# A two-layer trunk on one core: sums over channel tiles and every fifth tap added by accumulating transfers inside SBUF

## The chip, the cores and the metric

The kernel runs on one core of a Trainium2 chip. The metric is the device time of one execution in microseconds (us). The kernel before takes 1701.81 us, the median of three runs (1701.59 to 1702.53).

## The reference

The reference is a decoder trunk of two layers over 1024 tokens of 1024 channels, all in float32. Layer 0 mixes tokens by a causal depthwise convolution, layer 1 by a chunked spatial gate; behind each layer a per-layer embedding is added through a sigmoid gate, and one last RMSNorm ends it.

```python
for i in range(2):
    h = rmsnorm(x, norm_g[i])
    a, b, z = split(h @ w_in[i], 3)            # 3 x 2048 channels
    if i == 0:                                  # convolution layer
        y = a * sigmoid(b)
        y = causal_depthwise_conv(y, conv_w, 31 taps) + conv_b
        y = silu(layernorm(y))                  # over the 2048 channels
    else:
        y = gelu(a) * (w_s @ layernorm(gelu(b)) + b_s)   # in chunks of 128 tokens
    x = x + (y * silu(z)) @ w_out[i]
    x = x + sigmoid(rmsnorm(x) @ pl_gate_w[i]) * (p[i] @ pl_proj_w[i])
out = rmsnorm(x)
```

## The kernel before

Every product is made of three matmuls, since each float32 operand is cut into a head (`whi`, `ahi`, `phi`), rounded for the fast matmul, and a remainder (`wlo`, `alo`, `plo`): the head of one with the head and the remainder of the other, and the remainder of one with the head of the other (`three`, line 428). Heads are copied on ScalarE (ACT; line 314, or a cast on VectorE, DVE, at line 408), remainders are subtracted on GpSimd (POOL) or DVE (`tt`, lines 317 to 328). There are three buffers each for the heads and the remainders of weights.

In layer 0 the input product gives eight groups of two channel tiles of 128 channels by 1024 tokens. For each tile the product a * sigmoid(b) is written to `cin`, and `conv` (line 795) makes `y` from it with 31 taps. Eleven of the sixteen tiles are DVE's: each tap is one multiply-and-add into an accumulator in PSUM (`cv`, of which there is one, so these tiles come one after the other), and the last tap writes `y`. Five tiles (`POOL_CONV`) are POOL's: ACT makes the tap's product `m`, of which there are two buffers, and POOL adds it to `y` (line 815). Tile 0 is shared, with 15 of its taps on DVE.

The layernorm is over the channels, that is over partitions and tiles. So `stats` (line 836) adds each `y` to a running sum `acc` on POOL (`gather`, line 864); the squares of `y` less a first estimate of the mean (`cq`) are added likewise to `sq`. The sums over the first 15 tiles go through TensorE (PE) against a tile of 1/2048 (line 882: the mean for each token, in every partition) and against a column of ones (line 896: sums for each token). Tile 15's `y` and `cq` are then added to them in the same PSUM tiles. From the sums DVE and POOL make the deviation (`p_ln0`, line 911; the power on POOL, line 924), DVE writes it on diagonal tiles `dg`, and PE spreads it over the partitions (line 934). Then `p_g0` (line 938) reads `y` and silu(z) back from DRAM as `gt` and `zt`, subtracts the mean, multiplies by the deviation, takes silu, multiplies by `zt` and cuts the result into head and remainder for the output product. While the last convolution tiles are made, PE works on `p_proj` (line 722), the product of the embeddings `p`: for each layer it transposes rows `pr`, cuts them into `phi` and `plo`, and multiplies.

The order of all instructions comes from a planner (`Plan.schedule`, line 106): a simulation in which each engine takes the ready operation of the lowest rank whose buffers are free. An operation may name a second engine, which may take it from so many ns after it is ready on. With `pool=0`, `tt` gives an operation to POOL and lets DVE have it after `ALT_POOL`; this holds for operations made before `p_ln0`, and for the products with `zt`. A transfer issued by POOL is planned with 1400 ns on POOL, and as landed 5000 ns after its share of the bandwidth. The planner fixes only the order; on the chip each engine goes through its list and waits at each instruction for what it needs, so an engine that waits holds all that is behind. Transfers of weights, inputs and stored tiles are issued by the SP queue in the same manner, and in layer 1 POOL issues transfers that add a block of weights to a tile as it is loaded from DRAM (`add_load`, line 635).

Of the kernel before, what the change touches and what calls it, by code (L numbers as in the profile page):

```python
# [10 lines left out]
F32 = mybir.dt.float32  # L11
F32R = mybir.dt.float32r
AF = mybir.ActivationFunctionType
# [37 lines left out]
class Plan:  # L51
# [17 lines left out]
    def buf(self, make, tag=None):  # L69
        return Buf(make, tag)  # L70

    def op(self, eng, dur, fn, r=(), w=(), table=None, size=0, after=(), alt=None, port=False):


        o = Op()
        o.eng, o.dur, o.fn, o.table, o.size, o.alt, o.start, o.port = eng, dur, fn, table, size, alt, None, port
        o.seq = len(self.ops)
        o.prio = o.seq + self.offset
        deps = set(after)
        o.bufs, o.allocs = [], []  # L80
        for b in r:
            if b.writer is not None:
                deps.add(b.writer)
        for b in w:
            if b.writer is not None:
                deps.add(b.writer)
            deps.update(b.readers)
        for b in w:
            b.writer, b.readers = o, []
        for b in r:  # L90
            if b.writer is not o:
                b.readers.append(o)
        for b in {*r, *w}:
            b.users += 1
            o.bufs.append(b)
            if b.first is None:
                b.first = o
                if b.tag:
                    o.allocs.append(b)
        deps.discard(o)  # L100
        o.deps = deps
        o.nexts = []
        self.ops.append(o)
        return o
# [136 lines left out]
def trunk_kernel(ctx, tc, x, p, norm_g, w_in, w_out, conv_w, conv_b, conv_ln_g,  # L241
# [30 lines left out]
    def buf(tag, shape, dt, name):  # L272
        cnt[0] += 1
        n = f"{name}{cnt[0]}"
        rt, rn = real[tag]
        return plan.buf(lambda b: sb.tile(list(shape), dt, tag=rt, bufs=rn, name=n), tag)
# [40 lines left out]
    def tt(o, a, b, alu, n=CB, ps=False, pool=None, r=(), w=(), pool_first=False):  # L317

        dve = (DVE, (150 if ps else 250) + n * 1.042, lambda: nc.vector.tensor_tensor(  # L319
            out=o(), in0=a(), in1=b(), op=alu))  # L320
        pl = (POOL, 283 + n * 2.06, lambda: nc.gpsimd.tensor_tensor(out=o(), in0=a(), in1=b(), op=alu))  # L321
        if pool is None:
            return op(*dve, r, w, port=not ps)
        if pool == 0 and plan.dve_first is not None and not pool_first:
            return op(*dve, r, w, alt=(*pl, plan.dve_first), port=True)
        if pool == 0:
            return op(*pl, r, w, alt=(*dve, plan.alt_pool), port=True)
        return op(*dve, r, w, alt=(*pl, pool), port=True)
# [466 lines left out]
    def conv(c, ct):  # L795
        y = buf("y", (P, CW), F32, "y")

        def wt(i):
            return lambda: cw()[:, ct, i:i + 1]

        if ct in POOL_CONV:
            act(y, c, AF.Identity, CW, scale=wt(W - 1), bias=vcol(0, ct), r=[c, cw, vec], w=[y])
            own = W - DVE_TAPS.get(ct, 0)
            if own < W:
                a = plan.buf(lambda b: place["cv"][b.bank], "cv")
                ts_(lambda: a()[:, own:], lambda: c()[:, :S - own], wt(W - 1 - own), None, ALU.mult, None, CW, True,
                    r=[c, cw], w=[a])
                for s in range(own + 1, W):
                    stt(lambda s=s: a()[:, s:], lambda s=s: c()[:, :S - s], wt(W - 1 - s), lambda s=s: a()[:, s:],
                        ALU.mult, ALU.add, CW, r=[c, cw, a], w=[a])  # L810
            for s in range(1, own):
                m = buf("m", (P, CW), F32, "m")
                act(lambda m=m, s=s: m()[:, s:], lambda s=s: c()[:, :S - s], AF.Copy, CW, scale=wt(W - 1 - s),
                    r=[c, cw], w=[m])
                op(POOL, 283 + CW * 2.06, lambda m=m, s=s: nc.gpsimd.tensor_tensor(  # L815
                    out=y()[:, s:], in0=y()[:, s:], in1=m()[:, s:], op=ALU.add), [y, m], [y], port=True)
            if own < W:
                tt(lambda: y()[:, own:], lambda: y()[:, own:], lambda: a()[:, own:], ALU.add, CW, ps=True,
                   r=[y, a], w=[y])
            waiting.append((ct + POOL_LAG, ct, y))  # L820
        else:
            a = plan.buf(lambda b: place["cv"][b.bank], "cv")
            op(DVE, 70, lambda: nc.vector.tensor_copy(out=a()[:, 0:1], in_=vcol(0, ct)()), [vec], [a])
            ts_(lambda: a()[:, 1:], lambda: c()[:, :S - 1], wt(W - 2), vcol(0, ct), ALU.mult, ALU.add, CW, True,
                r=[c, cw, vec], w=[a])
            for s in range(2, W):
                stt(lambda s=s: a()[:, s:], lambda s=s: c()[:, :S - s], wt(W - 1 - s), lambda s=s: a()[:, s:],
                    ALU.mult, ALU.add, CW, r=[c, cw, a], w=[a])
            stt(y, c, wt(W - 1), a, ALU.mult, ALU.add, CW, r=[c, cw, a], w=[y])
            waiting.append((ct, ct, y))  # L830
        waiting.sort()
        while waiting and (waiting[0][0] <= ct or ct == KE - 1):
            _, i, v = waiting.pop(0)
            stats(i, v)
# [29 lines left out]
    def gather(name, y, n, col):  # L864

        acc = st["acc"]
        if n < KE - 1:
            prev = acc.setdefault(name, y)
            if n > 0:
                if n == 1 and name == "y":  # L870
                    acc[name] = w4("acc")
                a = acc[name]
                tt(a, prev, y, ALU.add, CW, pool=0, r=[prev, y], w=[a])
            if n < KE - 2:
                return
            y = acc.pop(name)
        if name == "y":
            for half in range(2):
                if n < KE - 1:
                    st.setdefault("mean", []).append(pm())  # L880
                ps = st["mean"][half]
                op(PE, 900, lambda ps=ps, half=half, y=y: nc.tensor.matmul(
                    out=ps(), lhsT=ones_e(), rhs=y()[:, half_of(half)], start=n < KE - 1, stop=n == KE - 1),
                    [ones_e, y], [ps])
        token_sums(y, col, n == KE - 1)
# [369 lines left out]
    with tc.manual_schedule():  # L1255
# [6 lines left out]
LATE = 300  # L1262
LATE_PROJ = 1500
ALT_ACT = 3000
ALT_POOL = 5000
A_POOL = 0
S_POOL = None
E_POOL = None
# [1 line left out]
NA = 2  # L1270
POOL_LAG = 2
ORDER0 = "0 1 z0 2 z1 3 z2 4 z3 5 z4 6 z5 7 z6 z7"
POOL_CONV = {0, 3, 6, 9, 12}
W4_BUFS = 32
CONV_BUFS = dict(cin=5, y=4, m=2, cq=2)
S2_BUFS = 14
# [10 lines left out]
PROJ_BACK = 0  # L1287
SUM_W = "raw"
SUM_B = SUM_AZ = False
_INS = ['x', 'p', 'norm_g', 'w_in', 'w_out', 'conv_w', 'conv_b', 'conv_ln_g', 'conv_ln_b',  # L1290
        'sgu_ln_g', 'sgu_ln_b', 'sgu_w', 'sgu_b', 'pl_norm_g', 'pl_gate_w', 'pl_proj_w', 'final_g']
_OUTS = [((1, 1024, 1024), 'float32')]
# [23 lines left out]
```

## Time and profile before

| | |
|---|---|
| median of 3 runs | 1701.81 us |
| profiled execution | 1703.15 us, its span 1701.4 us |
| mean granted clock of PE | 0.979 of 2.4 GHz |
| busy: PE, DVE, ACT, POOL | 96%, 72%, 45%, 42% of the span |
| POOL adds of taps (line 815) | 135, 326.7 us |
| DVE taps (line 331, `cv`) | 333, 423.1 us |
| DMA moved | 266.36 MB |

The span goes from the first to the last instruction of the profiled execution, and what lies around it is 1.75 us. Busy shares are means over stages that differ: layer 0's convolution fills the time up to about 635 us, and POOL's work lies mostly there. The waits of an engine are put down to the instruction that let it go on.

### The profile page before, as it was taken

To read this page: it belongs to the slowest core of one execution; us is meant where nothing else is said; L and a number is where in the kernel's file an instruction comes from. 1 tells how busy PE (TensorE), PEld (TensorE's weight loads), DVE (VectorE), ACT (ScalarE), POOL (GpSimd) and SP (SyncE) were. 2 spreads that over 40 slices of the span, in tenths; PEclk is the share of its full clock that TensorE was granted. 3 is DMA by queue.
4 is the path that set the end of the run, shared out by engine and by line. 5 is a ranking of instruction groups with operands and counts; after the bars stand their busy time and mean duration, and the time that the engine had idled before them with its cause. 6 is when DMAs were issued, how large, how long until landed. Compare 5 with 4: busy or idle time off the path is not lost.

```text
span 1701.4 us, 19540 instructions
## 1 busy us (share of the span) xinstructions
PE 1636.0 (96%) x7390; PEld 1349.9 (79%) x7390; DVE 1219.8 (72%) x1304; ACT 758.1 (45%) x944; POOL 712.0 (42%) x420
## 2 busy tenths in 40 slices
PE   6999999999999777999999899999999999999997
PEld 5888888888888655887888688888888888888886
DVE  4399989988989888475355684666666667798655
ACT  6445535445445735264345644333333334333652
POOL 3879999999999926031001411121111110010210
PEclk9999999999999886999999999999999999999999
DMA  5212222222224672483655958676676667845751
GB/s 168 88 62 87 86 76 83 79 75 75 81 85 144 235 241 93 140 291 138 209 199 187 234 148 213 179 173 168 165 180 162 169 164 209 298 161 173 253 216 75
DMA packets 165482, 266.36 MB, mean 157 GB/s; under 512 B 9694, under 2 KB 84558, under 8 KB 165388
## 3 DMA queue, kind: packets, MB, share of 16 engines
q1 hardware_dynamic: 143052, 237.85, 41.5%
q0 software_dynamic: 22336, 27.27, 10.2%
q8 instruction: 58, 0.95, 0.2%
q14 instruction: 36, 0.29, 0.1%
HBM read 206.36 MB, written 58.72 MB: 156 GB/s over the span
## 4 chain that ended last, share of the span: by engine, by line
PE 59%; DVE 1%; POOL 1%; issue 0%; ACT 0%; DVEq 0%; POOLq 0%; ACTq 0%
PE mm L432 41%; PE cv L432 15%; PE mm L1183 1%; PE mm L447 1%; PE cv L1183 0%; PE cv L447 0%; DVE gt L319 0%; DVE xr L319 0%; ACT ahi L314 0%; POOL sm L399 0%; DVE wlo L319 0%; POOL raw L636 0%; PE mm L934 0%; POOL sm L396 0%; DVE alo L319 0%
## 5 line engine op out<-in xcount | busy, mean ns | idle before, releaser
L314 ACT ACTIVATE whi<-raw 128x1024 fp32r<-128x1024 f32 (+1 forms) x198 | 205.9, 1042 | 520.4 <-PE mm L432 246.8
L331 DVE SCALAR_TENSOR_TENSOR cv<-cin,cw,cv 128x1022 f32<-128x1022 f32 (+28 forms) x333 | 423.1, 1271 | 10.0
L432 PE MATMUL mm<-alo,whi 128*128 128x512 f32 x1104 | 429.6, 389 | 0.0
L432 PE MATMUL mm<-ahi,whi 128*128 128x512 f32 x1056 | 413.6, 392 | 0.5 <-DVE alo L331 0.5
L432 PE MATMUL mm<-ahi,wlo 128*128 128x512 f32 x1056 | 411.0, 389 | 0.4 <-POOL wlo L321 0.4
L319 DVE TENSOR_TENSOR wlo<-raw,whi 128x1024 fp32r<-128x1024 f32 x183 | 232.5, 1273 | 161.3 <-ACT whi L314 160.8
L815 POOL TENSOR_TENSOR y<-y,m 128x1023 f32<-128x1023 f32 (+9 forms) x135 | 326.7, 2420 | 12.2 <-ACT m L314 6.1
L432 PE MATMUL mm<-whi,alo 128*128 128x512 f32 x704 | 275.8, 392 | 0.7 <-DVE alo L319 0.7
L432 PE MATMUL mm<-whi,ahi 128*128 128x512 f32 x656 | 258.8, 395 | 6.3 <-ACT ahi L314 5.1
L432 PE MATMUL mm<-wlo,ahi 128*128 128x512 f32 x656 | 257.3, 392 | 3.1 <-DVE wlo L319 3.1
L636 POOL DMA_DIRECT2D raw<-in_w_in_dram x52 | 65.9, 1276 | 427.8 <-DVE wlo L319 258.5
L432 PEld LDWEIGHTS mm<-alo,whi 128*128 128x128 f32 x1104 | 207.3, 188 | 42.5 <-issue 0.5
L432 PEld LDWEIGHTS mm<-ahi,wlo 128*128 128x128 f32 x1056 | 198.2, 188 | 42.1 <-POOL wlo L321 0.9
L432 PEld LDWEIGHTS mm<-ahi,whi 128*128 128x128 f32 x1056 | 198.3, 188 | 41.6 <-ACT whi L314 0.6
L432 PEld LDWEIGHTS mm<-whi,alo 128*128 128x128 f32 x704 | 133.1, 189 | 29.1 <-DVE alo L319 1.4
L432 PEld LDWEIGHTS mm<-whi,ahi 128*128 128x128 f32 x656 | 124.0, 189 | 33.7 <-ACT ahi L314 6.6
L314 ACT ACTIVATE m<-cin,cw 128x1023 f32<-128x1023 f32 (+9 forms) x135 | 147.4, 1128 | 0.0
L432 PEld LDWEIGHTS mm<-wlo,ahi 128*128 128x128 f32 x656 | 124.1, 189 | 29.2 <-DVE wlo L319 3.8
L321 POOL TENSOR_TENSOR wlo<-raw,whi 128x1024 fp32r<-128x1024 f32 (+1 forms) x49 | 109.1, 2229 | 43.0 <-ACT whi L314 40.3
L432 PE MATMUL cv<-whi,ahi 128*128 128x512 f32 x240 | 95.4, 397 | 5.5 <-ACT ahi L314 3.1
L432 PE MATMUL cv<-whi,alo 128*128 128x512 f32 x256 | 100.1, 391 | 0.0
L432 PE MATMUL cv<-wlo,ahi 128*128 128x512 f32 x240 | 94.1, 392 | 0.0
(203 smaller groups left out, 2044.9 us busy)
## 6 DMA issues: line engine op xcount, KB each, us to landing
raw<-in_w_in_dram SPq DMA_DIRECT2D x106, 512.0 KB, 4.1
raw<-in_w_out_dram SPq DMA_DIRECT2D x68, 512.0 KB, 4.6
raw<-in_w_in_dram POOLq DMA_DIRECT2D x52, 512.0 KB, 7.0
raw<-in_pl_gate_w_dram SPq DMA_DIRECT2D x32, 512.0 KB, 4.6
x<-xr SPq DMA_DIRECT2D x24, 512.0 KB, 6.9
xr<-x SPq DMA_DIRECT2D x24, 512.0 KB, 7.4
xr<-in_x_dram SPq DMA_DIRECT2D x16, 512.0 KB, 6.8
yd<-y SPq DMA_DIRECT2D x16, 512.0 KB, 2.9
```

The costliest lines, as they stand in the source:

```text
L314: nc.scalar.activation(out=o(), in_=i(), func=func, **kw)
L319: dve = (DVE, (150 if ps else 250) + n * 1.042, lambda: nc.vector.tensor_tensor(out=o(), in0=a(), in1=b(), op=alu))
L321: pl = (POOL, 283 + n * 2.06, lambda: nc.gpsimd.tensor_tensor(out=o(), in0=a(), in1=b(), op=alu))
L331: return op(DVE, 214 + n * 1.042, lambda: nc.vector.scalar_tensor_tensor(out=o(), in0=a(), scalar=s(), in1=b(), op0=op0, op1=op1), r, w)
L432: nc.tensor.matmul(out=acc(), lhsT=lw[a](), rhs=rw[b](), start=first and i == 0, stop=last and i == 2, skip_group_check=True)
L447: nc.tensor.transpose(out=ps()[:, t * P:(t + 1) * P], in_=rows[t]()[:, k * P:(k + 1) * P], identity=ident())
L636: op(POOL, 1400, lambda: nc.gpsimd.dma_start(out=raw(), in_=ap(), accum_op=ALU.add), [raw], [raw], size=2 * P * CW * 4)
L815: op(POOL, 283 + CW * 2.06, lambda m=m, s=s: nc.gpsimd.tensor_tensor(out=y()[:, s:], in0=y()[:, s:], in1=m()[:, s:], op=ALU.add), [y, m], ...
L1183: nc.tensor.matmul(out=ps()[:, t * P:(t + 1) * P], lhsT=v()[:, t, j * P:(j + 1) * P], rhs=wT()[:, ct * G // KE, :], start=True, stop=True)
```

## The change

Three things are changed. The running sums over channel tiles, `acc` and `sq`, are added by transfers that POOL issues, which read the new tile in SBUF and add it to the sum in SBUF (from the third tile to the thirteenth; the others stay adds). In POOL's convolution tiles a second tile `z` is begun by the second tap, which ACT writes straight into it, and every fifth tap from the third on is added to `z` by such a transfer; at the end `z` is added to `y`. And three numbers of the planner move: `ALT_POOL` from 5000 to 12000, and POOL's fifth tile from 12 to 13.

```diff
+            far = range(2, own, DMA_TAPS) if DMA_TAPS else ()
+            z = None
             for s in range(1, own):
+                if far and s == 1:
+                    z = buf("y", (P, CW), F32, "y2")
+                    act(lambda: z()[:, 1:], lambda: c()[:, :S - 1], AF.Copy, CW, scale=wt(W - 2), r=[c, cw], w=[z])
+                    continue
                 m = buf("m", (P, CW), F32, "m")
                 act(lambda m=m, s=s: m()[:, s:], lambda s=s: c()[:, :S - s], AF.Copy, CW, scale=wt(W - 1 - s),
                     r=[c, cw], w=[m])
+                if s in far:
+                    op(POOL, 1400, lambda m=m, s=s: nc.gpsimd.dma_start(
+                        out=z()[:, s:], in_=m()[:, s:], accum_op=ALU.add), [m, z], [z], size=2 * P * CW * 4)
+                    continue
                 op(POOL, 283 + CW * 2.06, lambda m=m, s=s: nc.gpsimd.tensor_tensor(
                     out=y()[:, s:], in0=y()[:, s:], in1=m()[:, s:], op=ALU.add), [y, m], [y], port=True)
+            if far:
+                tt(lambda: y()[:, 1:], lambda: y()[:, 1:], lambda: z()[:, 1:], ALU.add, CW, pool=0, r=[y, z], w=[y])
...
                 a = acc[name]
-                tt(a, prev, y, ALU.add, CW, pool=0, r=[prev, y], w=[a])
+                if DMA_ACC and 1 < n < KE - 3:
+                    op(POOL, 1400, lambda: nc.gpsimd.dma_start(out=a(), in_=y(), accum_op=ALU.add), [y, a], [a],
+                       size=2 * P * CW * 4)
+                else:
+                    tt(a, prev, y, ALU.add, CW, pool=0, r=[prev, y], w=[a])
...
-ALT_POOL = 5000
+ALT_POOL = 12000
...
-POOL_CONV = {0, 3, 6, 9, 12}
+POOL_CONV = {0, 3, 6, 9, 13}
...
+DMA_ACC = True
+DMA_TAPS = 5
```

Over the whole program POOL has 103 adds of taps in place of 135, 5 adds of `z` to `y`, 5 adds to `acc` and `sq` in place of 27, and 49 transfers (27 of taps, 22 of sums). DVE has no `cq` in place of 3, two remainders of weights less, and five casts of weight heads more; ACT has five heads less and as many products of taps as before.

In the order of DVE's instructions the place is the last write of `cin` (tile 15's input; the names with numbers are buffers). Before, ten taps of tile 13 and its `y` follow:

```order
L319 TENSOR_TENSOR cin_3613<-mm_69,sg_3512 128x512
L331 SCALAR_TENSOR_TENSOR cv<-cin_3158,cw,cv 128x1003
L331 SCALAR_TENSOR_TENSOR cv<-cin_3158,cw,cv 128x1002
L331 SCALAR_TENSOR_TENSOR cv<-cin_3158,cw,cv 128x1001
L331 SCALAR_TENSOR_TENSOR cv<-cin_3158,cw,cv 128x1000
L331 SCALAR_TENSOR_TENSOR cv<-cin_3158,cw,cv 128x999
L331 SCALAR_TENSOR_TENSOR cv<-cin_3158,cw,cv 128x998
L331 SCALAR_TENSOR_TENSOR cv<-cin_3158,cw,cv 128x997
L331 SCALAR_TENSOR_TENSOR cv<-cin_3158,cw,cv 128x996
L331 SCALAR_TENSOR_TENSOR cv<-cin_3158,cw,cv 128x995
L331 SCALAR_TENSOR_TENSOR cv<-cin_3158,cw,cv 128x994
L331 SCALAR_TENSOR_TENSOR y_3768<-cin_3158,cw,cv 128x1024
```

After the change, three taps of tile 12 and its `y` follow the same write:

```order
L408 CAST whi_3680<-raw_3312 128x1024
L319 TENSOR_TENSOR cin_3638<-mm_69,sg_3528 128x512
L331 SCALAR_TENSOR_TENSOR cv<-cin_3161,cw,cv 128x996
L331 SCALAR_TENSOR_TENSOR cv<-cin_3161,cw,cv 128x995
L331 SCALAR_TENSOR_TENSOR cv<-cin_3161,cw,cv 128x994
L331 SCALAR_TENSOR_TENSOR y_3723<-cin_3161,cw,cv 128x1024
```

Tiles 14 and 15 follow in both. So seven taps less stand behind the last write of `cin`, and the tile in work there is another.

On PE the place is the sums over the first 15 tiles (lines 882 and 896 before, 899 and 913 after). Before they stand in the middle of the second half's projections (heads `phi`, weight heads `whi`):

```order
L432 MATMUL mm_69<-wlo_3995,phi_4280 128x512
L432 MATMUL mm_69<-whi_3979,plo_4290 128x512
L882 MATMUL mm_68<-acc_1112,ones_e 128x512
L882 MATMUL mm_67<-acc_1112,ones_e 128x512
L896 MATMUL mm_71<-ones,acc_1112 128x1 x8
L896 MATMUL mm_71<-ones,sq_1182 128x1 x8
L432 MATMUL mm_69<-whi_3979,phi_4280 128x512
```

After the change they stand right behind the first half's projections, ahead of the transposes of the rows `pr`:

```order
L432 MATMUL mm_67<-wlo_3936,phi_4036 128x512
L432 MATMUL mm_67<-whi_3921,plo_4046 128x512
L899 MATMUL mm_66<-acc_1091,ones_e 128x512
L899 MATMUL mm_68<-acc_1091,ones_e 128x512
L913 MATMUL mm_71<-ones,acc_1091 128x1 x8
L447 MATMUL mm_69<-ident,pr_4152 128x128
L447 MATMUL mm_69<-ident,pr_4166 128x128
```

They moved 61 rows ahead (from row 2551 to row 2490 of PE's list); the token sums of `sq` follow eleven rows behind them.

On POOL the place is the last of its convolution tiles, around the adds of tile 12's `y` (`y_3768` before, where it is tile 13's) to the sums. Before:

```order
L815 TENSOR_TENSOR y_3188<-y_3188,m_3738 128x1014
L321 TENSOR_TENSOR acc_1112<-acc_1112,y_3768 128x1024
L815 TENSOR_TENSOR y_3188<-y_3188,m_3776 128x1013
L815 TENSOR_TENSOR y_3188<-y_3188,m_3800 128x1012
L321 TENSOR_TENSOR sq_1182<-sq_1182,cq_3829 128x1024
```

After the change (line 823 is a tap's transfer, line 887 that of a sum):

```order
L823 DMA y_3433<-m_3671 128x1012
L321 TENSOR_TENSOR wlo_3701<-raw_3312,whi_3680 128x1024
L826 TENSOR_TENSOR y_3380<-y_3380,m_3689 128x1011
L887 DMA acc_1091<-y_3723 128x1024
L321 TENSOR_TENSOR cq_3744<-y_3723,mA_1126 128x1024
L826 TENSOR_TENSOR y_3380<-y_3380,m_3734 128x1010
L887 DMA sq_1152<-cq_3744 128x1024
```

The adds to the two sums have become transfers, `cq`, which DVE made for this tile before, is now POOL's, and among the taps some are transfers to the second tile (`y_3433`).

## Rows read from the trace of the kernel before

**Rows 1.** Busy us by window: PE, PEld, DVE, ACT, POOL; clock, DMA share, GB/s
```profile
...
400.00:500.00 100.00, 100.00 (x443) 82.81 (x442) 88.43 (x72) 51.46 (x55) 97.08 (x42) 1.00 0.24 79
...
550.00:600.00 50.00, 41.15 (x167) 32.47 (x166) 42.27 (x40) 34.20 (x48) 45.36 (x19) 0.83 0.71 239
600.00:650.00 50.00, 34.27 (x144) 27.14 (x143) 43.55 (x47) 11.30 (x17) 8.73 (x4) 0.73 0.74 257
```

**Rows 2.** Waits of PE, 500 to 700 us: total us, times, longest us
```profile
...
PE mm L882 <- DVE y L331: 11.4, 1, 11.4
PE mm L447 <- DMA pr<-in_p_dram: 5.7, 2, 3.3
```

**Rows 3.** PE timeline: start us, us, engine line op, [idle before <-releaser]
```profile
...
622.54 0.39 PE L432 MATMUL mm<-whi,plo 128*128 128x512 f32 x1
634.30 3.78 PE L882 MATMUL mm<-y,ones_e 128*128 128x512 f32 x4 [11.37 <-DVE y L331]
637.88 3.41 PE L896 MATMUL mm<-ones,y 128*128 128x1 f32 x16
641.15 3.55 PE L896 MATMUL mm<-ones,cq 128*128 128x1 f32 x16
649.06 3.78 PE L934 MATMUL mm<-dg,ones 128*128 128x512 f32 x4 [4.36 <-DVE dg L337]
657.91 0.79 PE L432 MATMUL mm<-whi,ahi 128*128 128x512 f32 x1 [5.07 <-ACT ahi L314]
```

**Rows 4.** DVE's timeline from the last input tile to the gate tiles
```profile
...
511.12 12.93 DVE L331 SCALAR_TENSOR_TENSOR cv<-cin,cw,cv 128x1003 f32<-128x1003 f32 x10
...
530.88 3.11 DVE L319 TENSOR_TENSOR cq<-y,mA 128x1024 f32<-128x1024 f32 x1
...
581.00 1.28 DVE L331 SCALAR_TENSOR_TENSOR y<-cin,cw,cv 128x1024 f32<-128x1024 f32 x1
...
632.97 1.28 DVE L331 SCALAR_TENSOR_TENSOR y<-cin,cw,cv 128x1024 f32<-128x1024 f32 x1
636.41 8.01 DVE L319 TENSOR_TENSOR gt<-gt,mm 128x1024 f32<-128x1024 f32 x7 [2.17 <-PE mm L882]
```

**Rows 5.** POOL's timeline: last add of the sum over 15 tiles
```profile
...
597.09 2.42 POOL L321 TENSOR_TENSOR acc<-acc,y 128x1024 f32<-128x1024 f32 x1
```

**Rows 6.** DVE by shape, 0 to 640: busy us, mean ns, idle before
```profile
...
L319 DVE TENSOR_TENSOR wlo<-raw,whi 128x1024 fp32r<-128x1024 f32 x10 | 19.2, 1924 | 7.3 <-ACT whi L314 7.3
...
L408 DVE CAST whi<-raw 128x1024 fp32r<-128x1024 f32 x6 | 10.0, 1661 | 9.4 <-PE mm L432 9.4
```

**Rows 7.** Waits of DVE, 511 to 636 us
```profile
...
DVE wlo L319 <- ACT whi L314: 7.3, 4, 2.8
```

**Rows 8.** PE's timeline, second half's projections and the sums over 15 tiles
```profile
...
582.83 0.49 PE L447 MATMUL mm<-ident,pr 128*128 128x128 f32 x3
...
592.33 1.54 PE L447 MATMUL mm<-ident,pr 128*128 128x128 f32 x6 [2.38 <-DMA pr<-in_p_dram]
...
604.30 1.88 PE L882 MATMUL mm<-acc,ones_e 128*128 128x512 f32 x4
...
607.72 1.93 PE L896 MATMUL mm<-ones,sq 128*128 128x1 f32 x16
```

**Rows 9.** Busy time and PE clock by window, around the waits
```profile
...
614.00:623.00 9.00, 8.93 (x40) 7.06 (x38) 8.53 (x7) 3.70 (x8) 0.00 (x0) 1.00 0.80 257
634.00:650.00 16.00, 11.34 (x37) 8.73 (x38) 11.61 (x22) 1.06 (x1) 4.00 (x2) 0.50 0.74 266
```

**Rows 10.** Product tile m, 0 to 640: duration ns min/median/max
```profile
...
L314 ACT ACTIVATE m<-cin,cw x135: 1108/1130/1147, 50.6 to 587.7; 128x1023 f32<-128x1023 f32 x5, 128x1022 f32<-128x1022 f32 x5, 128x1021 f32<-128x1021 f32 x5, 128x1020 f32<-128x1020 f32 x5
L815 POOL TENSOR_TENSOR y<-y,m x135: 2281/2377/3362, 51.8 to 590.1; 128x1023 f32<-128x1023 f32 x5, 128x1022 f32<-128x1022 f32 x5, 128x1021 f32<-128x1021 f32 x5, 128x1020 f32<-128x1020 f32 x5
```

**Rows 11.** POOL transfers of line 636: duration ns min/median/max, landing us
```profile
...
L636 POOL DMA_DIRECT2D raw<-in_w_in_dram x52: 1194/1282/1712, 935.6 to 1419.9; - x52
...
DMA to landing us min/median/max: 5.6/7.0/10.8
```

## The prediction

> **What bounds the kernel now.** I read the busy time by stage first. TensorE (PE) is 100% busy from 400 to 500 us; it loses time from 550 to 650, where 25 of 100 us are idle and the granted clock falls to 0.83 and 0.73 [rows 1]. Nothing hidden under a full PE can be gained, so what decides is where the stretch after 550 ends. The waits of PE say what for: 11.4 us in one piece for y, the last convolution tile that VectorE (DVE) makes, and 5.7 us in two pieces for the second half's projection input [rows 2]. In PE's timeline the reader sees the place: the last projection matmul at 622.54, then nothing until y (tile 15) arrives at 634.3; three pieces of sums (3.78, 3.41, 3.55 us), a wait, the broadcast of the deviation at 649.06, and the first product of the next stage only at 657.91 [rows 3]. So this stage ends 23.7 us behind y (657.91 - 634.25). DVE's timeline shows why y is late: right behind the last input tile (cin) DVE goes on at 511.12, and it works 123 us, to 634.25 (632.97 + 1.28), on the rest of tile 13, on tiles 14 and 15, and on some adds and remainders between [rows 4]. GpSimd (POOL) is 97% busy [rows 1], but its sum over 15 tiles is there at 599.51 (597.09 + 2.42), 35 us before y [rows 5]: it is full, and not the last.
>
> **The change, part by part.** *DVE.* The order of work shows that behind the last cin write DVE has 7 fewer taps to do (3 in place of 10), one add less (cq, now POOL's), one remainder less (6 in place of 7), and one cast more. A tap takes 1.29 us (12.93 for 10), the cq took 3.11 [rows 4], a remainder 1.92 on the mean, a cast 1.66 [rows 6]: 9.0 + 3.1 + 1.9 - 1.7 = 12.3 us less. That DVE reaches the last cin no later I take from the order as well: between the last cin of one group and the first of the next it has two taps more and one remainder less, about zero. In that stretch it waits 7.3 us for weight heads [rows 7], which hang on PE and ScalarE (ACT), whose times don't move before 583. Laying the new order over those times, one tile 12 us earlier, I get 5 in place of 7.3. Bounds: 12 us of waits, if each now comes early, or none. I take 2 us gained, so y is done near 620, 14.3 us earlier; bounds 7.6 and 19.6.
>
> *PE.* The sums over the first 15 tiles stand 61 rows earlier, ahead of the transposes of the second half's projection input. PE gets there at 582.83. If they are ready it goes on: 1.88 us for the means and 1.9 each for two token sums [rows 8], transposes that can't end before about 593.5, since the last input came at 592.33 [rows 8], 96 matmuls at 0.226 us (100 us by 443) [rows 1] = 21.7, and 2 us at the lower clock behind the sums: about 617 to 620. So PE and y arrive together, and the wait of 11.4 us goes. What would be late next is PE itself, so a still earlier y would give nothing more.
>
> *Behind y.* PE arrives without having idled. The same sums, met at a granted clock of 1.00 (2.4 GHz), took 1.88 us for the means where they took 3.78 after the wait [rows 3, 8]; the clock of 614 to 623 is 1.00, that of 634 to 650 is 0.50 (1.2 GHz) [rows 9]. DVE now subtracts the mean from 6 gate tiles and not 7 before it turns to the sums: 8.01 / 7 = 1.1 us less [rows 4], and it starts 1 us earlier. A remainder (1.2 us) is put between the sums and the diagonal tiles; it lies beside POOL's power, for which DVE waits anyway, and costs up to 1.2 if that cover is gone. Together 2.2 us less.
>
> *POOL.* Up to its third tap on the last POOL tile it had 178 adds, and has 137 and 42 transfers. An add is 2.38 us [rows 10], and the only transfers that POOL issues in the trace hold it 1.28 us (1.19 to 1.71) [rows 11]: 41 x 2.38 - 42 x 1.28 = 44 us less. No accumulating transfer from SBUF to SBUF is in the trace. The nearest are those from DRAM, which land after 7.0 us (5.6 to 10.8) [rows 11]. Who waits: the next transfer on the same sum (five taps later, at least 9.5 us of adds between, so not at 7.0), and ACT, since a product tile m is held until landing and there are two. Then ACT (1.13 us) and POOL's add go one after the other, 1.1 us a tap lost for two taps in each of 27 tap transfers: 62 us at most, and I take half, since a remainder or another add often stands between. Against it stand the 44 us and 17 more, for the sum may come as late as 600 (below). POOL's last job, from tile 14's y on, is six adds, 14.3 us; tile 14 ended at 582.28 [rows 4] and now ends near 568, so the 15-tile sum comes at 582 to 583, just as PE asks. POOL makes two weight remainders more; PE holds three weight tiles of 10.9 us of work each (48 x 0.226), so a remainder a few us late costs nothing.
>
> A rule of the Trainium skill speaks against the transfers: "SBUF — State Buffer", section "SBUF: two separate sides", says that a DMA issued by GpSimd stalls while VectorE runs an instruction that takes the shared port pair, since the descriptors can't be written meanwhile. The trace bears it out weakly: 52 issues spread over 1.19 to 1.71 us [rows 11]. Were every issue as long as the longest row, POOL would lose 42 x 0.43 = 18 us of its 44, and the sum would stay.
>
> The sum: 14.3 + 2.2 = 16.5, of which I take 16, since later stages have waits of their own. The profiled execution took 1703.15 us: 1687.2. The median of the three runs is 1.34 lower: 1685.8, so 1686. With y at its bounds (7.6 or 19.6 us, the latter cut to about 17 by PE) the mechanism gives 9 to 19 us, 1683 to 1693.
>
> **The rivals.** *Half of it.* DVE's waits grow with its lead, or the 15-tile sum comes some us after 583, and PE stands there. For it: six POOL adds in a row after tile 14 have no slack. Against: one or two us there are hidden as long as PE isn't the later one. With DVE's waits at 12 us: 16 - 7 = 9 gained, and 2 to 4 us of standing more: 1693 to 1697.
>
> *POOL is no freer.* Each issue waits out one DVE instruction of 1.29 us [rows 4], since DVE hardly pauses: 49 x 1.29 = 63 us eat the 44 and all but nothing of the 17 is left, so the sum comes at about 600, as before. From 583 PE then has 34 us of rows before y's sums (its 40 us up to 622.9, less 5.7 of waits for inputs that have landed by then [rows 2]), so it reaches them at 634, where it stood: no change, 1702. [...] For it: nothing in the trace shows that kind of transfer. Against: all 52 issues end within 1.72 us [rows 11].
>
> *Slower: the 15-tile sum is late.* One place, PE's row of the sums over 15 tiles, and one price, a us of PE for each us after 600. At the longest landing seen, 10.8 us, three taps of a transfer go one after the other, 27 x 3.4 = 92 us with nothing between them; less the 61 us of slack (44 + 17) this is 31 late, less 2 behind y: 1702 + 29 = 1731. It decides from a loss of 61 / 27 = 2.3 us a transfer on, which is what 7.0 us of landing cost with nothing between. For it: POOL is in order, and ACT waits behind it. Against: 43 remainders and 15 other adds do stand between, and the DMA engines are at a share of 0.24 before 500 [rows 1].
>
> **How the numbers follow.** 0.2% is 3.4 us, about what this kernel's measurement can tell from no change. Forecast 0.61, half 0.16, no freer 0.09, slower 0.14. The first two are faster by over 3.4 us: 0.77; same 0.09; slower 0.14. The range leaves out the slower case and what lies below the forecast's edge: 1680 to 1701. The forecast's own range is 1683 to 1693.
>
> **What would show it.** Right: PE's wait for y gone or under 3 us, y's end at 617 to 623, the sums of the means near 1.9 us, the first product of the next stage at 639 to 644; issues of the new transfers at 1.2 to 1.4 us and landings under 9. Wrong: PE waiting several us for the sums over 15 tiles near 583; POOL idle before transfers by over 2 us each; ACT idle on m; PE idle between 400 and 500. A median above 1698 would mean that POOL's chain, not DVE's, sets this stage.

## The result, and the profile after

The changed kernel took 1686.98 us (median of 4 runs, 1684.04 to 1689.26), the kernel before 1702.17 us beside it: a ratio of 0.9902, with a 95% interval of 0.9885 to 0.9918. By the ratio that is 16.7 us (1702.17 x 0.0098) faster; the two medians are 15.2 us apart. 1686 had been forecast, with a range of 1680 to 1701. The profiled execution took 1689.26 us, the longest of the four, with a span of 1687.6. A second trace of the same kernel (e13 below, an execution of 1685.15 us) has the end of y at 615.81 and the first product of the next stage at 640.82, where this one has 617.34 and 643.17; so a difference of 2 us between two traces need not come from an edit. Two executions at a far lower granted clock, one of the changed kernel (2371.34 us, 0.65) and one of the kernel before (2000.09 us, 0.78), are left out.

The busy time of the changed kernel by window (PE, PEld, DVE, ACT, POOL; granted clock, DMA share, GB/s), against [rows 1]:

```profile
400.00:500.00 100.00, 100.00 (x442) 82.79 (x442) 90.80 (x75) 52.72 (x57) 88.73 (x45) 1.00 0.57 141
...
550.00:600.00 50.00, 43.52 (x188) 34.03 (x187) 44.83 (x41) 26.00 (x38) 30.75 (x14) 0.86 0.80 271
600.00:650.00 50.00, 35.42 (x138) 26.11 (x137) 42.21 (x46) 23.69 (x35) 15.66 (x6) 0.73 0.69 237
```

PE stays full where it was full. POOL is 89% busy from 400 to 500 us and no longer 97%, and the DMA share there has gone from 0.24 to 0.57. Now PE's waits from 500 to 700 us (total us, times, longest us), against [rows 2]:

```profile
PE mm L951 <- DVE dg L337: 8.8, 1, 8.8
PE cv L432 <- ACT ahi L314: 5.1, 1, 5.1
PE mm L432 <- ACT phi L314: 2.6, 2, 1.4
PE mm L432 <- DVE plo L319: 2.3, 3, 1.5
PE mm L913 <- POOL sq L321: 1.2, 1, 1.2
PE cv L432 <- DVE alo L319: 0.7, 1, 0.7
PE mm L447 <- DMA pr<-in_p_dram: 0.4, 1, 0.4
```

The wait of 11.4 us for y is gone, and so is nearly all of the 5.7 for the projection's input. The wait for the diagonal tiles behind y has doubled, from 4.36 us [rows 3] to 8.8. PE's timeline shows the same in place (start, duration, wait before):

```profile
582.75 1.88 PE L899 MATMUL mm<-acc,ones_e 128*128 128x512 f32 x4
584.47 1.84 PE L913 MATMUL mm<-ones,acc 128*128 128x1 f32 x16
...
588.40 3.47 PE L913 MATMUL mm<-ones,sq 128*128 128x1 f32 x16 [1.16 <-POOL sq L321]
...
618.12 1.88 PE L899 MATMUL mm<-y,ones_e 128*128 128x512 f32 x4
619.83 1.84 PE L913 MATMUL mm<-ones,y 128*128 128x1 f32 x16
621.53 2.52 PE L913 MATMUL mm<-ones,cq 128*128 128x1 f32 x16
...
634.32 2.07 PE L951 MATMUL mm<-dg,ones 128*128 128x512 f32 x2 [8.78 <-DVE dg L337]
636.18 1.92 PE L951 MATMUL cv<-dg,ones 128*128 128x512 f32 x2
643.17 0.79 PE L432 MATMUL cv<-whi,ahi 128*128 128x512 f32 x1 [5.07 <-ACT ahi L314]
```

The means and the token sums of `acc` over 15 tiles stand ahead of the second half's projections and wait for nothing; only the token sums of `sq` wait, 1.16 us, for POOL. The means over y take 1.88 us where they took 3.78 [rows 3]. The next stage's first product comes at 643.17 in place of 657.91: 14.7 us earlier, of which 13.8 are left in the span (1701.4 to 1687.6). In the second trace it is 17.1 us earlier, and the span 18.0 us shorter (1683.4). POOL and DVE around it, POOL first:

```profile
580.10 2.42 POOL L321 TENSOR_TENSOR acc<-acc,y 128x1024 f32<-128x1024 f32 x1
...
630.18 2.59 POOL L941 TENSOR_TENSOR sm<-sm,mhalf 128x8 f32<-128x8 f32 x1 [10.39 <-DVE sm L331]
```

```profile
616.06 1.28 DVE L331 SCALAR_TENSOR_TENSOR y<-cin,cw,cv 128x1024 f32<-128x1024 f32 x1
619.17 5.74 DVE L319 TENSOR_TENSOR gt<-gt,mm 128x1024 f32<-128x1024 f32 x5 [1.83 <-PE mm L899]
627.94 1.22 DVE L319 TENSOR_TENSOR gt<-gt,mm 128x1024 f32<-128x1024 f32 x1 [3.02 <-DMA gt<-yd]
...
630.02 1.22 DVE L319 TENSOR_TENSOR wlo<-raw,whi 128x1024 fp32r<-128x1024 f32 x1
632.80 1.66 DVE L337 TENSOR_SCALAR dg<-ident,sm 128x128 f32<-128x128 f32 x8 [1.57 <-POOL sm L941]
```

POOL's sum over 15 tiles ends at 582.52, 0.23 us before PE reads it; before, it ended at 599.51 [rows 5]. y ends at 617.34, 16.9 us earlier than at 634.25 [rows 4], and PE is there 0.78 us later. Behind y DVE stands 3.02 us for the sixth gate tile's load. The new transfers, one line each (issues: duration ns min/median/max; then of the same view the time to landing):

```profile
L823 POOL DMA_DIRECT2D y<-m x27: 830/877/1496, 52.5 to 558.8; - x27
...
DMA to landing us min/median/max: 4.5/5.1/8.5
```

```profile
L887 POOL DMA_DIRECT2D acc<-y x11: 853/870/1495, 187.8 to 515.1; - x11
L887 POOL DMA_DIRECT2D sq<-cq x11: 849/882/1192, 193.1 to 521.6; - x11
...
DMA to landing us min/median/max: 4.5/5.3/10.1
```

### The profile page after: what moved, and what is told of

It reads as the page before. It is cut to its first block, busy times and chain, and to the rows that moved or that the text cites. A ratio compares the mean times of both kernels' runs of the same rounds, so it can differ in the third digit from the quotient of the medians.

```text
span 1687.6 us, 19609 instructions
## 1 busy us (share of the span) xinstructions
PE 1632.8 (97%) x7390; PEld 1347.3 (80%) x7390; DVE 1211.3 (72%) x1304; ACT 754.1 (45%) x939; POOL 643.4 (38%) x425
## 4 chain that ended last, share of the span: by engine, by line
PE 60%; DVE 1%; issue 0%; ACT 0%; POOL 0%; DVEq 0%; POOLq 0%; ACTq 0%
PE mm L432 42%; PE cv L432 14%; PE mm L1200 1%; PE mm L447 1%; PE cv L447 1%; PE cv L1200 0%; DVE gt L319 0%; DVE wlo L319 0%; PE mm L1142 0%; DVE alo L331 0%; PE mm L951 0%; DVE alo L319 0%; DVE mx L331 0%; POOL sm L399 0%; DVE xr L319 0%
## 5 line engine op out<-in xcount | busy, mean ns | idle before, releaser
L319 DVE TENSOR_TENSOR wlo<-raw,whi 128x1024 fp32r<-128x1024 f32 x181 | 224.5, 1243 | 161.1 <-ACT whi L314 154.6
L432 PE MATMUL mm<-whi,alo 128*128 128x512 f32 x720 | 281.4, 391 | 0.0
L826 POOL TENSOR_TENSOR y<-y,m 128x1021 f32<-128x1021 f32 (+22 forms) x103 | 255.2, 2478 | 29.6 <-ACT m L314 27.6
L432 PE MATMUL mm<-whi,ahi 128*128 128x512 f32 x672 | 265.8, 396 | 0.0
L432 PE MATMUL mm<-wlo,ahi 128*128 128x512 f32 x672 | 263.0, 391 | 2.3 <-DVE wlo L319 2.3
L321 POOL TENSOR_TENSOR wlo<-raw,whi 128x1024 fp32r<-128x1024 f32 (+1 forms) x51 | 116.7, 2290 | 68.3 <-ACT whi L314 63.7
L314 ACT ACTIVATE m<-cin,cw 128x1022 f32<-128x1022 f32 (+28 forms) x130 | 141.0, 1128 | 1.2 <-POOL y L826 1.2
L432 PE MATMUL cv<-whi,ahi 128*128 128x512 f32 x224 | 89.0, 397 | 7.9 <-ACT ahi L314 5.4
L432 PE MATMUL cv<-whi,alo 128*128 128x512 f32 x240 | 95.0, 396 | 0.7 <-DVE alo L319 0.7
L432 PE MATMUL cv<-wlo,ahi 128*128 128x512 f32 x224 | 88.8, 396 | 0.8 <-DVE wlo L319 0.8
```

What stands on the lines that cost most here:

```text
L314: nc.scalar.activation(out=o(), in_=i(), func=func, **kw)
L432: nc.tensor.matmul(out=acc(), lhsT=lw[a](), rhs=rw[b](), start=first and i == 0, stop=last and i == 2, skip_group_check=True)
```

## The experiments

Each of the twelve was timed beside the kernel before, and the ratio is to that. The first three columns are read from the traces: the end of y, how long PE waited for it, and the first product of the next stage.

| kernel | y ends | PE waits for y | first product | median us | ratio, 95% interval |
|---|---|---|---|---|---|
| before | 634.25 | 11.4 | 657.91 | | 1 |
| changed | 617.34 | 0 | 643.17 | 1686.98 | 0.9902, 0.9885 to 0.9918 |
| e1 sums alone | 617.01 | 0 | 644.16 | 1687.69 | 0.9923, 0.9910 to 0.9935 |
| e2 taps alone | 632.19 | 16.4 | 655.86 | 1701.53 | 1.0001, 0.9992 to 1.0009 |
| e3 numbers alone | 623.50 | 2.3 | 646.55 | 1691.84 | 0.9951, 0.9939 to 0.9964 |
| e4 transfers alone | 637.80 | 14.0 | 661.49 | 1701.46 | 1.0000, 0.9987 to 1.0013 |
| e5 y 3 taps shorter | 613.24 | 0 | 642.49 | 1687.51 | 0.9920, 0.9908 to 0.9931 |
| e7 sum held back | 620.82 | 0 | 647.13 | 1690.22 | 0.9931, 0.9918 to 0.9943 |
| e8 gate tile moved | 616.00 | 0 | 639.86 | 1686.85 | 0.9911, 0.9898 to 0.9924 |
| e9 and remainder | 615.89 | 0 | 641.62 | 1689.87 | 0.9926, 0.9914 to 0.9938 |
| e10 order mended | 616.87 | 0 | 637.62 | 1683.12 | 0.9900, 0.9883 to 0.9917 |
| e11 one number | 630.65 | 10.1 | 653.91 | 1699.16 | 0.9991, 0.9982 to 1.0001 |
| e12 other number | 631.41 | 11.4 | 655.08 | 1700.14 | 0.9997, 0.9984 to 1.0010 |
| e13 changed, again | 615.81 | 0 | 640.82 | 1687.95 | 0.9919, 0.9898 to 0.9940 |

**Which part brings it.** Four kernels each hold a part of the change.

Sums alone, the changed kernel with `-DMA_TAPS = 5` `+DMA_TAPS = 0`:

> The changed kernel with the sums still moved by accumulating transfers, but all taps of GpSimd's convolution tiles added by GpSimd again. By the order VectorE's tail is nearly as short as in the changed kernel (65 taps behind the last input tile in place of 64), while GpSimd has 32 adds of 2.38 us more and 27 issues of 0.88 us and 5 adds less: 40 us. Theory (VectorE's tail sets the end of the stage, and GpSimd must be free enough to take the work from it): y is early, near 618, but the sum over 15 tiles comes 10 to 20 us after PE asks for it at 583, so that 1694 to 1702 us is expected. Rival (the tap transfers give GpSimd nothing, because the landing holds the two product buffers, and GpSimd waited 27.6 us for products): the same as the changed kernel or better, 1683 to 1688.

Taps alone, `-DMA_ACC = True` `+DMA_ACC = False`:

> The changed kernel with the tap transfers, but the 22 sums added by GpSimd again. The order leaves VectorE 73 taps, one remainder and two casts more behind the last input tile: 9 x 1.29 + 1.9 + 3.3 = 17 us, so y near 634, where it was before the change. Theory: 1700 to 1704, as before the change. Rival (it is the number of adds that GpSimd loses that counts, whatever VectorE does): two thirds of the gain, about 1692.

Numbers alone, both of these edits:

> The two planner numbers of the change alone (remainders stay longer on GpSimd; tile 13 on GpSimd in place of 12), no accumulating transfer. VectorE's tail is as short as in the changed kernel by the order (65 taps, 6 remainders, no squares' difference), but GpSimd has 73 us of adds more than in the changed kernel (54 adds of 2.38 us less 49 issues and 5 adds). Theory: y near 618, the sum over 15 tiles long after 600, PE stands for it, and the time is not better than before the change: 1702 to 1725. Rival (the planner's numbers bring the gain by themselves, the transfers nothing): 1685 to 1690.

Transfers alone, `-ALT_POOL = 12000` `+ALT_POOL = 5000` and `-POOL_CONV = {0, 3, 6, 9, 13}` `+POOL_CONV = {0, 3, 6, 9, 12}`:

> Both kinds of accumulating transfers, but the planner's numbers of the kernel before. By the order VectorE has 74 taps, 7 remainders and 4 casts behind the last input tile, 10 taps more than in the changed kernel: y near 634, as before the change. GpSimd is free early, its sum over 15 tiles is there when PE asks. Theory (VectorE's tail decides): 1700 to 1704, no gain. Rival (GpSimd's load was what held the stage): 1685 to 1690.

The transfers alone bring nothing, and show why. POOL of that kernel:

```profile
586.32 2.35 POOL L321 TENSOR_TENSOR acc<-acc,y 128x1024 f32<-128x1024 f32 x1 [13.23 <-DVE y L331]
```

POOL is free and stands 13.2 us for tile 14's y; DVE has 74 taps in its tail (71 before, 64 in the changed kernel), y ends at 637.80, and PE waits 14.0 us for it. So DVE's tail decides. The taps alone say the same (y at 632.19). The trace is of an execution of 1705.33 us, while the twelve of this kernel took 1696.73 to 1707.48; so some of the 3.6 us by which y is later than before the change may belong to that execution.

On the other two my theory missed the time. The numbers alone brought half of the gain (0.9951), where no gain or a loss had been expected. POOL's sum over 15 tiles did come late, but only at 605.64 (603.25 + 2.39), and the planner had put PE's rows that read it behind most of the projections (609.38), so nothing waited. And the sums alone came out like the whole change: PE asked for the sum at 589.22, after POOL had it (585.17 + 2.37 = 587.54), since the planner had again moved the rows. The rival's price for the sums alone was met; its reason, that tap transfers give POOL nothing, is not shown by that.

What the transfers add to the numbers is 6.2 us of y (623.50 to 617.34), and one line says where it comes from. DVE's instructions from the last input tile to the end of y, by shape (count, busy us, mean ns, idle before), first of the numbers alone and then of the changed kernel:

```profile
L319 DVE TENSOR_TENSOR wlo<-raw,whi 128x1024 fp32r<-128x1024 f32 x7 | 16.0, 2289 | 6.0 <-ACT whi L314 6.0
```

```profile
L319 DVE TENSOR_TENSOR wlo<-raw,whi 128x1024 fp32r<-128x1024 f32 x6 | 9.1, 1521 | 6.3 <-ACT whi L314 5.0 <-PE mm L447 1.3
```

Up to y both make six remainders; in the kernel with the numbers alone they take 14.8 us (16.0 less the seventh, of 1.22, which lies behind y), here 9.1: 5.7 of the 6.2 us; the rest (taps, waits, a cast and the last input tile) nearly cancels out. A remainder that starts while a POOL add runs takes up to 3.38 us, one that starts while none runs 1.22, and then it is the POOL instruction behind it that takes longer. DVE's rows and POOL's, of the numbers alone:

```profile
571.87 3.38 DVE L319 TENSOR_TENSOR wlo<-raw,whi 128x1024 fp32r<-128x1024 f32 x1 [2.54 <-ACT whi L314]
...
623.42 1.22 DVE L319 TENSOR_TENSOR wlo<-raw,whi 128x1024 fp32r<-128x1024 f32 x1
```

```profile
571.81 2.37 POOL L826 TENSOR_TENSOR y<-y,m 128x1002 f32<-128x1002 f32 x1
574.12 3.40 POOL L321 TENSOR_TENSOR cq<-y,mA 128x1024 f32<-128x1024 f32 x1
...
623.58 3.27 POOL L321 TENSOR_TENSOR cq<-y,mA 128x1024 f32<-128x1024 f32 x1 [10.71 <-DVE y L331]
```

The remainder at 571.87 starts 0.06 us behind the start of a POOL add and ends about 1.1 us behind that add's end; POOL's next, at 574.12, is longer by what the remainder still took. The remainder at 623.42 starts ahead of POOL's instruction and keeps to 1.22 us; that instruction takes 3.27 us, and 2.36 in the changed kernel (at 617.42). The taps, between which these stand, keep to 1.25 to 1.29 us in both kernels. The sums alone, whose POOL still adds every tap, need 9.5 us for their six remainders; so the transfers of the sums are enough to shorten them. The orders of these kernels differ too, and no price per add follows from this.

**One number at a time**, on the kernel before: `-ALT_POOL = 5000` `+ALT_POOL = 12000`, and apart from it `-POOL_CONV = {0, 3, 6, 9, 12}` `+POOL_CONV = {0, 3, 6, 9, 13}`.

> The kernel before the change with one of the planner's numbers alone: remainders, sums and differences stay longer on GpSimd, tile 12 stays on GpSimd, no accumulating transfer. By the order VectorE has 4 taps and one difference less behind the last input tile and 3 casts more: 5.2 + 3.1 - 5.0 = 3.3 us less, and GpSimd is fuller, so that its adds meet VectorE's remainders more. Theory (count of VectorE's tail): y at 631 to 634, 1699 to 1702. Rival (each of the two numbers brings half of what both bring): 1697.

> The kernel before the change with the other number alone: tile 13 on GpSimd in place of tile 12, no accumulating transfer. By the order VectorE has one tap less and two casts more behind the last input tile: 2 us more. Theory (count of VectorE's tail): y at 634 to 637, 1701 to 1704. Rival (each of the two numbers brings half): 1697.

Neither is told from no change (0.9991 and 0.9997); y ends at 630.65 and 631.41. Together they give 8 us. So the gain is not a sum over edits: only with both does the order leave DVE 65 taps and six remainders in its tail (with one number alone 67 or 70 taps, and seven remainders). For tile 13 alone y came 2.6 us ahead of the earliest counted (634). Its trace shows that the last input tile was written 2.6 us earlier than before the change (at 508.56 in place of 511.20); why it was is open.

**What is last behind y.** Leave out three taps of DVE's last tile (`SKIP = 3`):

```diff
             for s in range(2, W):
+                if ct == KE - 1 and s > W - 1 - SKIP:
+                    op(DVE, 214 + CW * 1.042, lambda: None, [c, cw, a], [a])
+                    continue
```

> The changed kernel without the last three taps of VectorE's last convolution tile (they are left out of what is computed; the order of all else is the same), so that y ends some 3.8 us earlier, near 613.5. Theory (behind y the stage is no longer set by y but by TensorE, which reaches the sums over y at 618.1 without a wait, and by the sixth gate tile, which lands at 627.9): within 1 us of the changed kernel, 1686 to 1688. Rival (VectorE's tail still sets the end of the stage, one to one): 3.8 us less, 1683.

DVE's row behind y:

```profile
619.26 5.75 DVE L319 TENSOR_TENSOR gt<-gt,mm 128x1024 f32<-128x1024 f32 x5 [6.02 <-PE mm L902]
```

y ended at 613.24, 4.1 us earlier than in the changed kernel, and nothing followed: DVE stood 6.02 us for PE's means, and the first product moved by 0.7, less than the two traces of the changed kernel differ. So the prediction's sentence holds that a still earlier y gives nothing more. Then the other chain, POOL's sum, was held back by a subtraction and an addition of the same tile ahead of its last add (`HOLD = 1`):

```diff
-                    tt(a, prev, y, ALU.add, CW, pool=0, r=[prev, y], w=[a])
+                    o = tt(a, prev, y, ALU.add, CW, pool=0, r=[prev, y], w=[a])
+                    if name == "y" and n == KE - 2:
+                        def held(add=o.fn, y=y):
+                            for f in (ALU.subtract, ALU.add) * HOLD:
+                                nc.gpsimd.tensor_tensor(out=a(), in0=a(), in1=y(), op=f)
+                            add()
+                        o.fn = held
```

> The changed kernel with two more GpSimd adds of 2.4 us right ahead of the last add of the sum over 15 tiles (the tile is subtracted and added again), unknown to the planner: the sum comes at 587.3 in place of 582.5, 4.6 us after TensorE asks for it. Theory A, that of the prediction (the sum comes just in time, and TensorE's rows from 583 to the sums over y set the end): 3 to 5 us more than the changed kernel, 1690 to 1692. Theory B (the sixth gate tile's landing at 627.9 sets the end, and hides what TensorE loses): TensorE reaches the sums over y near 622, VectorE has subtracted from five gate tiles near 629; 1 to 2 us more, 1688 to 1689. Rival (slack everywhere): no difference.

PE's row of that sum:

```profile
587.83 3.74 PE L905 MATMUL mm<-acc,ones_e 128*128 128x512 f32 x4 [5.37 <-POOL acc L321]
```

PE waited 5.37 us for the sum, and the first product came at 647.13, 4.0 us later than in the changed kernel (6.3 later than in its second trace); the median rose by 2 to 3 us against it (1690.22 to 1687.95 and 1686.98; the intervals of the ratios touch or overlap, so the size rests on the traces). Theory A holds. Theory B falls for a reason worth keeping: the sixth gate tile did not land at its old time but 4 us later (DVE's row at 631.88 in place of 627.94), because on SP's queue its load stands right behind three stores of projection rows (`pr`), which hang on PE's projections: it was issued at 620.74 in place of 617.26. y was later too, by 3.5 us, since DVE's remainders of the projection input stand in its queue and hang on PE (DVE waited 3.7 us in one piece for `phi`).

**The wait for the gate tile.** In the order of DVE's instructions the subtraction from the sixth gate tile (and, behind it, the seventh) was moved behind the second gate product (`KEEP = 5`), and in a second kernel the remainder too (`REST = True`). `st["gate"]` and `st["mul"]` list the gate tiles' subtractions and products:

```diff
+    muls = [o for o in order if o in st["mul"]]
+    j = order.index(muls[1])
+    late = [o for o in order[j - 60:j] if o.eng == DVE and (o in st["gate"][KEEP:] or REST and o.seq > muls[1].seq
+            and o not in st["gate"] and o.port)]
...
+    for o in reversed(late):
...
+        order.remove(o)
+        order.insert(order.index(muls[1]) + 1, o)
```

> The changed kernel with one VectorE instruction moved in the order: the subtraction of the mean from the sixth gate tile, for which VectorE waited 3.0 us at 624.9, stands behind the second gate product and no longer ahead of the deviation's chain. Theory (that wait, and the 1.2 us of the instruction, are on the path): the diagonal tiles come 4.2 us earlier, the first product of the next stage near 639; 1682 to 1684. Rival (the gate tiles' landings only move the wait further on, or TensorE's sums end too late for it): 1686 to 1688.

> As the kernel before this one (sixth gate subtraction behind the second gate product), and the remainder that VectorE makes at 630.0 behind it as well. GpSimd's power took 2.59 us beside that remainder, and 1.66 in the kernel before the change, where nothing stood beside it. Theory (the remainder stands in the power's way): 1 us less than the kernel before this one, 1681 to 1683, and a power of about 1.7 us. Rival (the power is as long without it): no difference to the kernel before this one.

The diagonal tiles came at 627.23 (before this edit 632.80, and 630.45 in the second trace), but the first product only at 639.86, 1.0 us ahead of the second trace, and the medians gained nothing. ACT's rows of the first of these kernels say where the gain went:

```profile
632.12 2.23 ACT L314 ACTIVATE gt<-gt,vec 128x512 f32<-128x512 f32 x3 [7.61 <-DVE gt L319]
636.64 2.22 ACT L314 ACTIVATE gt<-gt,vec 128x512 f32<-128x512 f32 x3 [2.30 <-DVE gt L319]
638.77 1.04 ACT L314 ACTIVATE ahi<-gt 128x1024 fp32r<-128x1024 f32 x1
```

ACT takes its work in order, three gate tiles' activations before the first head `ahi`; the third tile's product now stood behind the moved subtractions, ACT waited 2.30 us, and PE waits 7.3 us for the head in place of 5.1. With the remainder moved to the same place it is worse (10.1 us). On the power the theory held: 1.67 us with no remainder beside it, 2.59 with one. The second kernel's trace is of an execution of 1684.05 us, while its other five took 1688.9 to 1690.7; what those did differently is open.

So the order was mended with ACT in view: the remainder goes behind the diagonal tiles, where DVE waits for PE's broadcast, and the subtractions behind the fifth gate product:

```diff
+    j = order.index(muls[4])
+    late = [o for o in order[j - 80:j] if o.eng == DVE and o in st["gate"][5:]]
...
+    for group, behind in ((rest, st["last_dg"]), (late, muls[4])):
+        for o in reversed(group):
+            order.remove(o)
+            order.insert(order.index(behind) + 1, o)
```

> The changed kernel with VectorE's order behind y mended: the remainder stands behind the diagonal tiles, where VectorE waits for TensorE's broadcast anyway, and the subtractions from the sixth and seventh gate tile behind the fifth gate product. Theory (the earlier attempts lost their gain because ScalarE, in order, waited for the third and later gate products behind the moved instructions): diagonal tiles near 626 to 628, ScalarE's first head tile near 637, TensorE's first product of the next stage near 638 and its second, for which it needs the remainder of the gate tile, at 641; 3.5 to 5 us less than the changed kernel, 1682 to 1684. Rival (the landings of the gate tiles, or what follows, take it back again): 1686 to 1688.

PE's rows of it:

```profile
628.77 2.07 PE L951 MATMUL mm<-dg,ones 128*128 128x512 f32 x2 [3.71 <-DVE dg L337]
630.64 1.92 PE L951 MATMUL cv<-dg,ones 128*128 128x512 f32 x2
637.62 0.79 PE L432 MATMUL cv<-whi,ahi 128*128 128x512 f32 x1 [5.07 <-ACT ahi L314]
641.90 0.80 PE L432 MATMUL cv<-whi,alo 128*128 128x512 f32 x1 [3.05 <-DVE alo L319]
```

The first product comes at 637.62 and not 643.17 (640.82 in the second trace), the product of the remainder `alo` at 641.90 and not 645.12 (642.76), and the median is the lowest of all, 1683.12. The theory's times were met within 1 us (638, 641, 1682 to 1684).

> The changed kernel once more, beside the others on the same chip, to place the mended order and the kernel with the sums alone (0.9923 of the time before the change) against it. Theory (the transfers of taps add nothing that TensorE can use, since y is early enough with the sums alone): 0.991 to 0.993 of the time before. Rival (they add 2 to 4 us of their own): 0.988 to 0.990.

The changed kernel beside it took 1687.95 (0.9919 to the mended order's 0.9900). The intervals overlap (0.9898 to 0.9940 and 0.9883 to 0.9917): the traces show 3.2 to 5.6 us at the first product and 0.9 to 3.2 at that of the remainder, but the times alone don't yet tell the two apart. Nor do they tell the changed kernel from the sums alone, so a gain from the tap transfers of their own is not shown.

## Why the prediction was right, step by step

- **DVE's tail.** The step held, and y came 16.9 us earlier where 14.3 were taken. By the traces: 9.1 us less of taps, 3.1 for `cq`, 2.3 of remainders, 2.9 of waits, the last input tile 1.5 earlier, less 2.0 for the cast. What I had put at nothing is the last input tile. The waits for weight heads went from 7.3 to 5.0 us, as laid out; what the sum left out is 2.7 us of waits for `phi`, which went, and 2.1 us for PE, which came in. A remainder was counted at 1.92 us, the mean over the whole convolution; in this stretch seven took 11.4 us and six now take 9.1.
- **PE and y arrive together.** Forecast 617 to 620 for both; 618.12 and 617.34. The wait went, and shortening y further gave nothing.
- **Behind y.** This step failed. From y's end to the first product it took 25.8 us (643.17 - 617.34), where 23.7 were before and 21.5 were forecast: 2.2 us longer and not 2.2 shorter, 4.4 us the wrong way, against 2.6 us more from y. In the second trace it took 25.0 us. So the gain at the first product is 16.9 - 2.2 = 14.7 us and not 16.5; the ratio, at 16.7 us (interval 14.0 to 19.6), doesn't tell these apart. That the forecast time was met within 1 us is thus in part luck, since the two errors partly cancel. From the diagonal tiles on it took 10.37 us before and after (647.54 to 657.91, 632.80 to 643.17), so the loss lies ahead of them. The means did take 1.88 us, but DVE started on the gate tiles only 0.3 us earlier behind y and not 1. Six gate subtractions in place of seven saved nothing, since the sixth waited 3.02 us for its load (2.22 in the second trace), which I had not looked at. And the remainder beside POOL's power was not free: the power took 2.59 us in place of 1.66, in both traces. In the windows of the changed kernel the DMA share is 1.00 before that load lands, and PE idles between its sums and the broadcast, at a granted clock of 0.50 (1.2 GHz):

```profile
614.00:623.00 9.00, 9.00 (x51) 7.30 (x50) 7.10 (x7) 3.00 (x5) 2.36 (x1) 0.98 1.00 293
625.00:634.00 9.00, 0.54 (x2) 0.00 (x0) 4.36 (x14) 1.54 (x2) 2.59 (x1) 0.50 0.84 279
```

- **POOL.** The sum over 15 tiles came at 582.52, forecast 582 to 583, and the held-back sum shows that it had no slack. The sizes behind it were off, to the good: an issue took 0.88 us (1.28 forecast) and landing 5.1 (7.0), though one landing, of 10.1 us, was beyond the 9 that I had named as a sign. The loss on product tiles was about as taken: POOL waited 31.8 us for them (27.6 before adds, 4.2 before transfers) where it waited 6.1 before, 25.7 more, against 31 taken.
- **The rivals.** No freer falls: no issue is longer than 1.50 us, though DVE hardly pauses. The late sum falls as well, since PE found the sum ready. So does the half, which gave 1693 to 1697 where 1686.98 was measured. What I did not see is that half of the gain needs no transfer at all.
- **The rule on the port pair.** The Trainium skill, "SBUF — State Buffer", section "SBUF: two separate sides", was weighed for the issues alone, and the trace shows no such stall there (no issue is longer than 1.50 us). The same section says that a VectorE instruction with two inputs in SBUF and a GpSimd instruction that reads SBUF exclude each other for their whole length. The traces agree: the remainders took 1.22 us alone and up to 3.38 beside an add, the power 1.67 and 2.59. By the traces this is how the transfers move y: DVE's remainders meet fewer POOL adds.

## What to carry to other kernels

When work is taken from an engine that is full but not last, nothing is gained until the planner hands it work from the engine that is last: test the room and its use apart. Before counting on an earlier end, follow every queue behind it: the load, the store ahead of that load, and the in-order engine that waits for the third instruction and not the first. And an instruction put into another engine's wait is free only if the two don't hold each other up, as the remainder and the power did here.

## What the runs showed of the hardware

An accumulating transfer of about 512 KB from SBUF to SBUF cost POOL 0.88 us of issue (0.83 to 1.50) and landed after 4.5 to 10.1 us, while DVE was 91% busy (400 to 500 us). A POOL add of 2.4 us that started behind a DVE remainder became 3.4 us, a remainder that started behind an add 3.38 in place of 1.22, while DVE's 333 taps stayed between 1.25 and 1.29 us.
